# Scores of two heads at once in the two row halves of the array, in the first mixer of a three-mixer block

## The chip, the cores and the metric

The kernel runs on one core of a Trainium2 chip. A core has five engines that run side by side: TensorE (PE in the profile, with its weight loads as PEld), VectorE (DVE), ScalarE (ACT), GpSimd (POOL) and SyncE (SP), which here only issues DMAs. The metric is the device time of one execution in microseconds, lower is better.

## The reference

Two transformer blocks are chained over 512 tokens of width 1024, in float32. The change touches the first mixer alone, which has eight heads of forgetting attention ("fox") and eight heads of chunked attention with a relative bias ("chk"), all 64 wide. What it must compute per head:

```
def fox_attention(q, k, v, log_f):
    ...
        s = jnp.einsum('bqhd,bkhd->bhqk', qb, k).astype(jnp.float32) * scale
        s = s + cq[..., :, None] - cum[..., None, :]
        mask = k_pos[None, :] <= q_pos[:, None]
        p = jax.nn.softmax(jnp.where(mask, s, -jnp.inf), axis=-1)
        return jnp.einsum('bhqk,bkhd->bqhd', p.astype(v.dtype), v)
...
def even_mixer(h, w_in, b_forget, rel_bias, w_out):
    ...
    o = jnp.concatenate([o_a.reshape(b, s, W_FOX), o_b.reshape(b, s, W_CHK)], axis=-1)
    return o @ w_out
```

After it come a squared-ReLU MLP, a second mixer (stick-breaking and latent attention), a second MLP, a third mixer (differential and sparse attention) and a gated MLP. None of these is edited, but all share the planner that is described below.

## The kernel before, in words

Every float32 operand is kept as a pair: a high part, rounded to the short float format that TensorE takes, and a low part, the rest (`split`, one ScalarE and one VectorE instruction). A product of two pairs takes three matmuls: high by high, high by low, low by high. A matrix product `gemm` walks over weight blocks of 128 by 1024: a DMA brings the block (`wr`), `split` makes `wh` and `wl`, and 24 matmuls of 512 columns use it. These are the `psg<-h,wh` and `psg<-h,wl` rows; every matmul is preceded by its own weight load of 128 columns.

The first mixer works on pairs of heads. For each pair, `qk` makes q and k of both heads, each as one tile of 128 rows (head 0 in rows 0 to 63, head 1 in rows 64 to 127) by two parts by 512 tokens. For the scores, `to_stack` moves q by four DMAs into a tile `QS`, in which one head's high part stands in rows 0 to 63 and its low part in rows 64 to 127. `to_dup` moves k by four DMAs into two tiles `KK`, one for each head, with that head's k twice, one copy under the other. One matmul over 128 rows then adds two of the products, so that two matmuls (with k's high and low part) give a head's scores. Per head there are four of them in turn, for token blocks i = 0 to 3, with n = 128(i+1) columns.

`softmax` runs per block: VectorE adds the bias and takes the minimum (tile `x`), ScalarE does the exponential, VectorE the reciprocal, and GpSimd scales. `turn` transposes the four blocks on TensorE (`psp<-cst,x`), `av` multiplies by v (`pso<-pt,V`), and `fold` adds the two halves. The heads of a pair follow each other.

Nothing is issued in the order in which it is written. A `Recorder` notes every operation, `cost` gives each a price from a table, and `schedule` plays the five engines forward with these prices, with the buffers of each tile name (`BUFS`, `PBUFS`: two banks `s` for scores, three `g` for the products) and with priorities. The order that comes out is issued, so every instruction has the line of the issuing helper, L372, and groups are told apart by their tiles. TensorE runs its matmuls in that fixed order.

Pieces of later work (`fill`, `later`) stand between the steps of a pair, so that TensorE has matrix products to do while a softmax is on its way.

Of the kernel before, what the change touches and what calls it, by code (L numbers as in the profile page):

```python
# [14 lines left out]
AF = mybir.ActivationFunctionType  # L15
ALU = mybir.AluOpType
# [4 lines left out]
NT = 4  # L21
# [224 lines left out]
def size(ap):  # L246
    return math.prod(n for _, n in ap.ap[1:])


class Recorder:  # L250
# [71 lines left out]
    def cost(self, op):  # L322
        n = max(size(a) for a in op.acc[1] + op.acc[0])
        out = op.args[0]
        psum = any(str(a.space).endswith("PSUM") for a in op.acc[0])
        e = op.eng
        k = sum(isinstance(a, AP) for a in op.args[2:]) + sum(isinstance(a, AP) for a in op.kw.values())
        if op.name == "dma_start":
            return 450 if str(op.args[1].space).endswith("DRAM") else 625
        if e == "tensor":  # L330
            n = size(out)
            if op.name == "transpose":
                return 107
            if op.args[2].dtype == F32:
                return max(4 * n / 2.4, 428)
            return n / 2.4 + 2.5
        if e == "scalar":
            return 93 + 0.833 * n - (40 if psum else 0) + 93 * k
        if e == "vector":
            if op.name == "reciprocal":  # L340
                return 67 + 6.3 * n
            if op.name in ("memset", "tensor_copy") or (op.name == "tensor_scalar" and not psum):
                return 67 + 0.53 * n + 58 * k
            if op.name == "scalar_tensor_tensor":
                return 67 + 1.05 * n + 60 * (k - 1)
            return 67 + 1.05 * n
        if op.name == "tensor_scalar":
            return 160 + 0.836 * n + 83 * k
        if op.name == "affine_select":
            return 90 + 1.2 * n  # L350
        if op.name == "memset":
            return 36 + 0.83 * n
        return 958 if n <= 4 else 60 + 2.3 * n
# [37 lines left out]
    def schedule(self):  # L391
# [30 lines left out]
        while len(order) < len(ops):  # L422
            best = None
            for e in engs:
                if avail[e]:
                    s = clock[e]
                elif pend[e]:
                    s = max(clock[e], pend[e][0][0])
                else:
                    continue  # L430
                if best is None or s < best[0]:
                    best = (s, e)
            if best is None:
                raise RuntimeError("no instruction is ready: " + str({t: len(w) for t, w in waiting.items() if w}))
            now, e = best
            while pend[e] and pend[e][0][0] <= now:
                k = heapq.heappop(pend[e])[1]
                heapq.heappush(avail[e], (ops[k].prio, k))
            op = ops[heapq.heappop(avail[e])[1]]
            need = [t for t in op.tiles if t not in held]  # L440
            short = None
            for t in need:
                tag = self.tag[t]
                if not free[tag] or turn[t] != at[tag]:
                    short = tag
            if short is not None:
                waiting[short].append(op.n)
                continue
            late = max([free[self.tag[t]][0] for t in need], default=0.0)
            if late > now:  # L450
                heapq.heappush(pend[e], (late, op.n))
                continue
            for t in need:
                tag = self.tag[t]
                heapq.heappop(free[tag])
                held.add(t)
                at[tag] += 1
                for k in waiting[tag]:
                    heapq.heappush(pend[ops[k].eng], (now, k))
                waiting[tag] = []  # L460
            cost = op.cost
            if e == "tensor":
                stat = self.region(op.args[1])
                if stat != last:
                    cost = max(cost, 107)
                last = stat
            elif op.name == "activation" and TABLE.get(op.args[2], table) != table:
                table = TABLE[op.args[2]]
                cost += 1280
            end = now + cost  # L470
            clock[e] = end
            lat = self.LAT[e]
            if op.name == "tensor_tensor_reduce":
                lat = dict.fromkeys(lat, 425)
            if op.name == "dma_start":
                nbytes = 4 * math.prod(n for _, n in op.args[0].ap)
                dma = max(dma, end + 650) + nbytes / 360
                end = dma
            op.end = end
            order.append(op)  # L480
            for k in op.succ:
                o = ops[k]
                o.ready = max(o.ready, end + lat.get(o.eng, 0))
                o.left -= 1
                if not o.left:
                    heapq.heappush(pend[o.eng], (o.ready, o.n))
            for t in op.tiles:
                users[t] -= 1
                done_at[t] = max(done_at.get(t, 0.0), end + 200)
                if not users[t]:  # L490
                    tag = self.tag[t]
                    heapq.heappush(free[tag], done_at[t])
                    for k in waiting[tag]:
                        heapq.heappush(pend[ops[k].eng], (now, k))
                    waiting[tag] = []
# [7 lines left out]
class Net:  # L503
# [201 lines left out]
        self.nc.vector.tensor_tensor(x, ps, x, ALU.add)  # L705


    def scaled_pair(self, ps, rbc):
        t = self.tl("G", [128, 512])
        self.nc.vector.tensor_tensor(t, ps, rbc, ALU.mult)  # L710
        ab = self.pair("AB")
        self.split(ab, t)
        return ab

# [30 lines left out]
    def softmax(self, i, passes, bias, gate=None):  # L745

        nc = self.nc
        n = 128 * (i + 1)
        s = self.scores(i, passes)
        p = self.tl("x", [128, 512])  # L750
        m = self.small(4)
        nc.vector.tensor_tensor_reduce(p[:, :n], s[:, :n], bias(i), scale=1.0, scalar=3e38,
                                       op0=ALU.add, op1=ALU.min, accum_out=m[:, 0:1])
        nc.scalar.activation(p[:, :n], p[:, :n], AF.Exp, scale=-1.0, bias=m[:, 0:1], accum_out=m[:, 1:2])
        nc.vector.reciprocal(m[:, 2:3], m[:, 1:2])
        if gate == "raw":
            return p, m[:, 2:3]
        nc.gpsimd.tensor_scalar(p[:, :n], p[:, :n], m[:, 2:3], 1.0 if gate is None else gate(i), ALU.mult, ALU.mult)
        return p

    def turn(self, ps_list):

# [44 lines left out]
    def vhead(self, vt, u):  # L807
        return lambda j: vt[j][:, u].rearrange("p a d -> p (a d)")

    def qk(self, key, mov, rq, rk, tags="gg"):  # L810
        res = [None, None]

        def evac(m, ps):
            ab = self.scaled_pair(ps, rq if m == 0 else rk)
            res[m] = ab

        self.gemm(key, mov, evac, tags)
        return res
# [43 lines left out]
    def even_mixer(self):  # L862
        nc = self.nc
        rbc, rbcq = self.finish_norm([("rbc", 1.0), ("rbcq", -0.125)])
        h = self.h
# [6 lines left out]
        vt = self.v_tiles("fox_v0", h, self.rcol, gates, self.first)  # L872
# [6 lines left out]
        ps = self.psum("s")  # L879
# [36 lines left out]
        for kind, mk in (("fox", fox_bias), ("chk", chk_bias)):  # L916
            for t in range(4):
                if not (kind == "fox" and t == 0) and t % 2 == 0:
                    vt = self.v_tiles(f"{kind}_v{t // 2}", h, self.rcol)
                q, k = self.qk(f"{kind}_qk{t}", h, rbcq, rbc, "op" if kind == "fox" and t == 0 else "gg")  # L920
                qs = self.to_stack(q)
                kk = self.to_dup(k)
                if kind == "chk":
                    if t == 0:
                        half = self.out_part("out_ab0", ops[:4])
                    self.fill(half, OUT0[t], FILL0)
                ob = self.T()
                for u in range(2):
                    passes = [(qs[:, u], kk[u][:, 0]), (qs[:, u], kk[u][:, 1])]
                    self.soft_head(passes, mk(2 * t + u), self.vhead(vt, 2 * (t % 2) + u), ob, u)  # L930
                ops.append(self.finish_pair(ob))
        self.rec.flush()
        self.out_proj("out_ab1", ops[4:], "mlp0")
# [834 lines left out]
```

## Time and profile before

| what | value |
|---|---|
| median of 3 runs | 2084.16 us (2082.13 to 2088.24) |
| the profiled execution's own time | 2076.13 us |
| its span, first to last instruction | 2074.1 us |
| TensorE busy | 2017.1 us, 97% |
| VectorE, ScalarE, GpSimd busy | 55%, 43%, 19% |
| mean granted TensorE clock | 0.993 |

The profiled execution is 8 us shorter than the median of the timed runs, with 2 us of it outside the span. Matmul durations in the profile overlap, since a matmul is still draining when the next has begun; the pace of TensorE is therefore read from the distance between start times, not from durations.

### The profile page before, as it was taken

How to read it: one execution, taken by the hardware profiler on the slowest of the kernel's cores; microseconds unless marked ns; L12 is line 12 of the kernel's file. 1: busy time of each engine (PE TensorE's matmuls, PEld its weight loads, DVE VectorE, ACT ScalarE, POOL GpSimd, SP SyncE). 2: the span in 40 equal slices, each digit the busy share in tenths (PEclk: the TensorE clock that was granted, in tenths of full speed). 3: DMA queues.
4: the chain of work that ended last, by engine and by line, in shares of the span. 5: the costliest groups of instructions: out<-in, count | busy, mean ns of one | idle time of the engine just before them, and what ended most of it. 6: DMA issues, size and time to landing. Idle time of an engine off the chain costs nothing. (4 is left out here: it accounts for less than half of the span.)

```text
span 2074.1 us, 27228 instructions
## 1 busy us (share of the span) xinstructions
PE 2017.1 (97%) x9958; PEld 1683.7 (81%) x9958; DVE 1131.8 (55%) x2033; ACT 895.1 (43%) x1621; POOL 396.5 (19%) x524
## 2 busy tenths in 40 slices
PE   8999999999999999999999999989999999999998
PEld 7888878888888877778888888867788888888887
DVE  5667853434445576774434344766786644333334
ACT  5556542322335555653323243543685543222224
POOL 2343210000022463220000014211340221011013
PEclk9999999999999999999999999999999999999999
DMA  6445623333344315632333334473213222223232
GB/s 199 129 129 154 198 83 100 94 99 97 97 139 127 102 62 131 180 115 92 102 93 101 94 122 135 122 182 116 71 42 112 92 101 92 101 93 102 91 102 82
DMA packets 80293, 231.98 MB, mean 112 GB/s; under 512 B 11424, under 2 KB 15392, under 8 KB 80160
## 3 DMA queue, kind: packets, MB, share of 16 engines
q1 hardware_dynamic: 80160, 230.25, 36.8%
q8 instruction: 78, 1.28, 0.3%
q14 instruction: 55, 0.45, 0.1%
HBM read 183.04 MB, written 10.49 MB: 93 GB/s over the span
## 5 line engine op out<-in xcount | busy, mean ns | idle before, releaser
L372 PE MATMUL psg<-h,wh 128*128 128x512 f32 x2688 | 848.4, 393 | 0.9 <-ACT h L372 0.6
L372 ACT ACTIVATE wh<-wr 128x1024 fp32r<-128x1024 f32 (+3 forms) x313 | 326.3, 1042 | 846.0 <-PE psg L372 672.9
L372 PEld LDWEIGHTS psg<-h,wh 128*128 128x128 f32 x2688 | 503.3, 189 | 102.0 <-ACT h L372 1.5
L372 PE MATMUL psg<-h,wl 128*128 128x512 f32 x1344 | 528.9, 393 | 1.2 <-DVE wl L372 1.0
L372 DVE TENSOR_TENSOR wl<-wr,wh 128x1024 fp32r<-128x1024 f32 (+3 forms) x313 | 384.7, 1229 | 59.9 <-ACT wh L372 58.7
L372 PEld LDWEIGHTS psg<-h,wl 128*128 128x128 f32 x1344 | 253.6, 189 | 53.9 <-DVE wl L372 3.1
L372 PE MATMUL psg<-KK,wh 128*128 128x512 f32 (+1 forms) x788 | 237.8, 383 | 0.4 <-DVE V L372 0.2
L372 DVE TENSOR_TENSOR x<-psg,x 128x512 f32<-128x512 f32 (+1 forms) x120 | 78.2, 654 | 281.8 <-PE psg L372 281.7
L372 POOL TENSOR_TENSOR acc<-acc,T 128x512 f32<-128x512 f32 (+1 forms) x50 | 72.9, 1457 | 775.7 <-issue 627.3
L372 PE MATMUL psg<-V,wh 128*128 128x512 f32 (+1 forms) x672 | 205.7, 387 | 1.1 <-DVE G L372 1.1
L372 PEld LDWEIGHTS psg<-KK,wh 128*128 128x128 f32 x788 | 146.3, 188 | 29.5 <-ACT o L372 0.6
L372 PE MATMUL psg<-KK,wl 128*128 128x512 f32 (+1 forms) x394 | 150.8, 383 | 0.0
L372 PEld LDWEIGHTS psg<-V,wh 128*128 128x128 f32 x672 | 125.6, 188 | 27.3 <-ACT wh L372 1.2
L372 DVE SCALAR_TENSOR_TENSOR T<-psg,rbc 128x512 f32<-128x512 f32 x64 | 44.2, 691 | 167.2 <-PE psg L372 166.8
L372 ACT ACTIVATE x<-x,sm 128x128 f32<-128x128 f32 (+1 forms) x192 | 106.6, 558 | 54.7 <-DVE sm L372 53.9
L372 PE MATMUL psg<-V,wl 128*128 128x512 f32 (+1 forms) x336 | 129.9, 387 | 0.0
L372 PE MATMUL psg<-o,wh 128*128 128x512 f32 x384 | 126.2, 397 | 0.8 <-ACT wh L372 0.5
L372 PE MATMUL psg<-wh,h 128*128 128x256 f32 (+2 forms) x560 | 114.5, 292 | 6.6 <-ACT wh L372 6.6
L372 PE MATMUL pso<-pt,V 128*128 128x128 f32 (+3 forms) x432 | 108.8, 340 | 3.4 <-ACT pt L372 1.9
L372 POOL TENSOR_SCALAR x<-x,sm 128x128 f32<-128x128 f32 (+1 forms) x112 | 65.9, 594 | 174.6 <-DVE sm L372 122.8
L372 PEld LDWEIGHTS psg<-wh,h 128*128 128x128 f32 x560 | 92.4, 194 | 8.4 <-ACT wh L372 6.6
L372 POOL TENSOR_TENSOR T<-T,rbc 128x512 f32<-128x512 f32 x22 | 39.2, 1782 | 280.5 <-ACT T L372 280.5
(263 smaller groups left out, 2667.6 us busy)
## 6 DMA issues: line engine op xcount, KB each, us to landing
wr<-in_w_dram SPq DMA_DIRECT2D x302, 512.0 KB, 3.5
KK<-AB SPq DMA_DIRECT2D x48, 256.0 KB, 5.4
QS<-AB SPq DMA_DIRECT2D x48, 128.0 KB, 4.0
x<-xs SPq DMA_DIRECT2D x24, 256.0 KB, 3.3
xs<-P SPq DMA_DIRECT2D x16, 256.0 KB, 3.9
xs<-x SPq DMA_DIRECT2D x16, 256.0 KB, 2.0
h<-AB SPq DMA_DIRECT2D x16, 256.0 KB, 4.1
KK<-AB SPq DMA_DIRECT2D x32, 128.0 KB, 2.3
```

Of the source, the lines that this page charges most:

```text
L372: op.inst = getattr(getattr(nc, op.eng), op.name)(*op.args, **op.kw)
```

## The change

The stacked copies of q and k go. `qk` writes q's pair straight into a tile `QS` and k's into a tile `KK`, and each head's matmuls read their own 64 rows: head 0 rows 0 to 63, head 1 rows 64 to 127. Each token block then takes three matmuls over 64 rows per head instead of two over 128, written with the two heads in turn. Both heads' softmaxes are written side by side, with i from 3 down to 0, and share tiles `x`; the transposes of both heads come after them. The planner's prices change too: a matmul of pairs counts 32 columns' time beyond its own n columns where it counted 6, one over 64 rows counts half of that, and this holds for the whole program.

```diff
@@ cost
-            return n / 2.4 + 2.5
+            return (n + 32) / (4.8 if op.args[1].ap[0][1] == 64 else 2.4)
@@ schedule
-                    cost = max(cost, 107)
+                    cost = max(cost, 107 if op.args[1].ap[0][1] > 64 else 53)
@@ scaled_pair
-    def scaled_pair(self, ps, rbc):
+    def scaled_pair(self, ps, rbc, tag="AB"):
...
-        ab = self.pair("AB")
+        ab = self.pair(tag)
@@ new functions
+    HALF = ((0, 0), (0, 1), (1, 0))
+
+    def scores_two(self, i, q, k):
...
+        s = [self.psum("s"), self.psum("s")]
+        for a, (x, y) in enumerate(self.HALF):
+            for u in range(2):
+                r = slice(64 * u, 64 * u + 64)
+                nc.tensor.matmul(s[u][:, :n], q[r, x, 128 * i:128 * i + 128], k[r, y, :n], start=(a == 0), stop=(a == 2))
+        return s
...
+    def soft_pair(self, q, k, bias, v, dst):
...
+        P = [[None] * NT, [None] * NT]
+        bias = [b() for b in bias]
+        for i in (3, 2, 1, 0):
+            s = self.scores_two(i, q, k)
+            for u in range(2):
+                if i == 3:
+                    P[u][3] = self.tl("x", [128, 512])
...
+                self.soften(i, s[u], P[u][i], bias[u])
+        for u in range(2):
+            pt = self.turn(P[u])
+            o = self.psum("o")
+            self.av(o, pt, v[u])
+            self.fold(o, dst, u)
@@ qk
-    def qk(self, key, mov, rq, rk, tags="gg"):
+    def qk(self, key, mov, rq, rk, tags="gg", to=("AB", "AB")):
...
-            ab = self.scaled_pair(ps, rq if m == 0 else rk)
+            ab = self.scaled_pair(ps, rq if m == 0 else rk, to[m])
@@ even_mixer
-                q, k = self.qk(f"{kind}_qk{t}", h, rbcq, rbc, "op" if kind == "fox" and t == 0 else "gg")
-                qs = self.to_stack(q)
-                kk = self.to_dup(k)
+                q, k = self.qk(f"{kind}_qk{t}", h, rbcq, rbc, "op" if kind == "fox" and t == 0 else "gg", ("QS", "KK"))
...
-                for u in range(2):
-                    passes = [(qs[:, u], kk[u][:, 0]), (qs[:, u], kk[u][:, 1])]
-                    self.soft_head(passes, mk(2 * t + u), self.vhead(vt, 2 * (t % 2) + u), ob, u)
+                self.soft_pair(q, k, [lambda u=u: mk(2 * t + u) for u in range(2)],
+                               [self.vhead(vt, 2 * (t % 2) + u) for u in range(2)], ob)
```

`soften` is the old `softmax` without its scores and its tile: the same VectorE, ScalarE and GpSimd instructions.

How the planner's order moves shows best on TensorE in the last pair of heads of the mixer. There `psg` rows are the output product that fills in, and `pss` rows the scores. In the kernel before, the two matmuls of a token block stand together and all take 128 rows:

```order
L372 MATMUL pss_693<-KK_680,QS_679 128x128 x2
L372 MATMUL pss_696<-KK_680,QS_679 128x256 x2
L372 MATMUL psg_614<-o_357,wh_616 128x512
L372 MATMUL psg_614<-o_357,wl_617 128x512
L372 MATMUL psg_614<-o_430,wh_616 128x512 x2
L372 MATMUL pss_699<-KK_680,QS_679 128x384 x2
L372 MATMUL pss_702<-KK_680,QS_679 128x512 x2
```

In the changed kernel the same place, the widest block (n = 512, tile 649 for head 0 and 650 for head 1), reads so:

```order
L372 MATMUL pss_649<-KK_636,QS_630 128x512
L372 MATMUL pss_650<-KK_636,QS_630 128x512
L372 MATMUL psg_568<-o_339,wl_571 128x512
L372 MATMUL psg_568<-o_406,wh_570 128x512 x2
L372 MATMUL psg_568<-o_406,wl_571 128x512
L372 MATMUL psg_573<-o_191,wh_570 128x512 x2
L372 MATMUL pss_649<-KK_636,QS_630 128x512
L372 MATMUL pss_650<-KK_636,QS_630 128x512
L372 MATMUL pss_649<-KK_636,QS_630 128x512
L372 MATMUL pss_650<-KK_636,QS_630 128x512
L372 MATMUL psg_573<-o_191,wl_571 128x512
```

Here the heads alternate, as they are written, but 128-row products stand between the runs. At the other widths, the heads do not alternate. This is the first pair, also in the changed kernel, where tile 150 is head 0 and 151 head 1 at n = 384, and 158 and 159 the same at n = 256:

```order
L372 MATMUL pss_150<-KK_136,QS_130 128x384 x3
L372 MATMUL psg_192<-h_95,wh_194 128x512
L372 MATMUL psg_192<-h_95,wl_195 128x512
L372 MATMUL pss_151<-KK_136,QS_130 128x384 x3
L372 MATMUL psg_192<-h_97,wh_194 128x512 x2
L372 MATMUL psg_192<-h_97,wl_195 128x512
L372 MATMUL psg_192<-h_99,wh_194 128x512 x2
L372 MATMUL psg_192<-h_99,wl_195 128x512
L372 MATMUL pss_158<-KK_136,QS_130 128x256 x3
```

The three matmuls of one head stand together and those of the other head come later. Counted over the mixer, the changed kernel has 192 score matmuls in 64 runs with other matmuls between them: 10 runs in which the heads alternate (six of four matmuls, four of two), 4 lone ones at n = 512, and 50 runs of three or six, in each of which one head's matmuls of a width stand together.

On SP's queue the moves stood between the loads of weights, as here in the first pair of the kernel before (`wr` are weight blocks):

```order
L372 DMA QS_137<-AB_130 64x512 x2
L372 DMA wr_271<-in_w_dram 128x1024
L372 DMA QS_137<-AB_130 64x512 x2
L372 DMA wr_274<-in_w_dram 128x1024
L372 DMA KK_138<-AB_136 64x1024 x2
L372 DMA KK_139<-AB_136 64x1024 x2
```

In the changed kernel the `QS` and `KK` rows of the first mixer are gone from this queue and the `wr` rows follow each other.

## Rows read from the trace of the kernel before

**Rows 1.** The page: busy us of each engine, share of the span, instructions.
```profile
PE 2017.1 (97%) x9958; PEld 1683.7 (81%) x9958; DVE 1131.8 (55%) x2033; ACT 895.1 (43%) x1621; POOL 396.5 (19%) x524
```

**Rows 2.** Busy time by window; columns PE, PEld, DVE, ACT, POOL, clock, DMA share, GB/s.
```profile
29.00:266.00 237.00, 231.19 (x1309) 196.65 (x1308) 163.47 (x387) 131.75 (x296) 83.20 (x150) 1.00 0.55 152
...
280.00:640.00 360.00, 359.47 (x1637) 299.39 (x1636) 154.18 (x176) 118.87 (x152) 13.57 (x8) 1.00 0.32 101
```

**Rows 3.** What PE waited for in the first mixer, 29 to 266 us.
```profile
PE pss L372 <- DMA KK<-AB: 3.2, 3, 1.4
PE psp L372 <- POOL x L372: 1.3, 3, 0.8
PE pso L372 <- ACT pt L372: 0.6, 1, 0.6
PE psp L372 <- DVE pt L372: 0.2, 1, 0.2
PE psg L372 <- DVE wl L372: 0.2, 1, 0.2
```

**Rows 4.** PE in order of time, first mixer: start, us, tiles, rows*columns, shape.
```profile
223.28 0.70 PE L372 MATMUL pss<-KK,QS 128*128 128x128 f32 x4 [0.65 <-DMA KK<-AB]
223.81 0.40 PE L372 MATMUL psg<-o,wh 128*128 128x512 f32 x1
...
224.73 0.97 PE L372 MATMUL pss<-KK,QS 128*128 128x384 f32 x4
225.54 0.40 PE L372 MATMUL psg<-o,wl 128*128 128x512 f32 x1
```

**Rows 5.** PE in order of time, in the first MLP.
```profile
300.52 0.62 PE L372 MATMUL psg<-h,wh 128*128 128x512 f32 x2
300.97 0.39 PE L372 MATMUL psg<-h,wl 128*128 128x512 f32 x1
```

**Rows 6.** PE in order of time, third mixer: one 32-row matmul among 128-row ones.
```profile
1534.99 0.39 PE L372 MATMUL psg<-h,wh 128*128 128x512 f32 x1
1535.32 0.49 PE L372 MATMUL pso<-P,vcmp 32*128 32x512 f32 x1
1535.73 0.50 PE L372 MATMUL psg<-h,wl 128*128 128x512 f32 x1
1536.07 0.63 PE L372 MATMUL psg<-h,wh 128*128 128x512 f32 x2
```

**Rows 7.** PEld, the weight loads, at the same place.
```profile
1534.88 0.19 PEld L372 LDWEIGHTS psg<-h,wh 128*128 128x128 f32 x1
1535.31 0.18 PEld L372 LDWEIGHTS pso<-P,vcmp 32*128 32x128 f32 x1 [0.24 <-ACT x L372]
1535.73 0.19 PEld L372 LDWEIGHTS psg<-h,wl 128*128 128x128 f32 x1 [0.24 <-issue]
```

**Rows 8.** PE in order of time, third mixer: two 32-row matmuls together.
```profile
1517.35 0.45 PE L372 MATMUL pso<-pt,V 128*128 128x256 f32 x3
1517.73 0.73 PE L372 MATMUL pso<-P,vcmp 32*128 32x512 f32 x2
1518.39 0.98 PE L372 MATMUL psp<-cst,x 128*128 128x128 f32 x7
1519.13 0.48 PE L372 MATMUL pss<-X,rbcq 128*128 128x512 f32 x1
```

**Rows 9.** PE in order of time: two 62-row transposes among 128-row ones.
```profile
1449.34 0.38 PE L372 MATMUL psp<-cst,x 128*128 128x128 f32 x2
1449.65 0.33 PE L372 MATMUL psg<-cst,P 62*128 62x62 f32 x2
1449.92 0.44 PE L372 MATMUL psp<-cst,x 128*128 128x128 f32 x2
1450.11 0.48 PE L372 MATMUL pss<-KK,QS 128*128 128x512 f32 x1
```

**Rows 10.** The score matmuls of the first mixer, by their tile KK, to 280 us.
```profile
L372 PE MATMUL pss<-KK,QS x128: 220/336/497, 44.3 to 228.8; 128*128 128x128 f32 x32, 128*128 128x256 f32 x32, 128*128 128x384 f32 x32, 128*128 128x512 f32 x32
```

More of the change, by code (lines that the diff above doesn't have):

```diff
@@ L759, in softmax, with soften @@
         return p
+    HALF = ((0, 0), (0, 1), (1, 0))
+    def scores_two(self, i, q, k):
+        nc = self.nc
+        n = 128 * (i + 1)
+        s = [self.psum("s"), self.psum("s")]
[4 more added lines that the diff above has]
+        return s
+    def soften(self, i, s, p, bias):
+        nc = self.nc
+        n = 128 * (i + 1)
+        m = self.small(4)
+        nc.vector.tensor_tensor_reduce(p, s[:, :n], bias(i), scale=1.0, scalar=3e38,
+                                       op0=ALU.add, op1=ALU.min, accum_out=m[:, 0:1])
+        nc.scalar.activation(p, p, AF.Exp, scale=-1.0, bias=m[:, 0:1], accum_out=m[:, 1:2])
+        nc.vector.reciprocal(m[:, 2:3], m[:, 1:2])
+        nc.gpsimd.tensor_scalar(p, p, m[:, 2:3], 1.0, ALU.mult, ALU.mult)
+    def soft_pair(self, q, k, bias, v, dst):
[6 more added lines that the diff above has]
+                    P[u][3] = self.tl("x", [128, 512])
+                elif i == 2:
+                    t = self.tl("x", [128, 512])
+                    P[u][2], P[u][0] = t[:, 0:384], t[:, 384:512]
+                elif i == 1:
+                    if u == 0:
+                        t1 = self.tl("x", [128, 512])
+                    P[u][1] = t1[:, 256 * u:256 * u + 256]
+                self.soften(i, s[u], P[u][i], bias[u])
[4 more added lines that the diff above has]
+            self.fold(o, dst, u)
     def turn(self, ps_list):
```

## The prediction

> **What bounds the kernel now.** I read the page first. TensorE is busy 97% of the span and no other engine over 55% [rows 1], so what a change adds to or takes from TensorE's queue is what the end moves by, as long as TensorE has other work in its waits. Then the table of windows, to see whether that holds where the change is made. The first mixer, from 29 to 266 us, has TensorE busy for 231.19 of 237.00 us; in the MLP behind it, 359.47 of 360.00 [rows 2]. The reader is to see that only 5.8 us of this mixer are open. The list of waits says what they are: 3.2 us for the moves of k, and 1.3, 0.6, 0.2 and 0.2 us for GpSimd, ScalarE and VectorE [rows 3]. So 5.5 us is all that freeing TensorE from others can give here. The rest must come from its own pace, which I read from start times.
>
> **The third pass.** The mixer has 128 score matmuls over 128 rows, 32 of each width [rows 10]. In the order of time, four of them (two of 128 and two of 256 columns) take 223.81 - 223.28 = 0.53 us, and four of 384 and 512 take 225.54 - 224.73 = 0.81 us [rows 4]. A head thus needs 1.34 us, and sixteen heads 21.4 us. Half the rows do not halve a matmul's columns. With three matmuls per block where two stood, 192 at the same pace are 32.2 us: **+10.7 us**.
>
> **Two heads at a time.** What comes off this is only what the two row halves really do at once. No row of this trace has two matmuls in different halves next to each other, so I bound it. Nothing comes off, if they queue; at most, each neighbouring couple takes the time of one. The order of the changed kernel has ten alternating runs, six of four matmuls and four of two, all of 512 columns: 16 couples. The pace of a 512-column matmul is 0.225 us (two in 0.45 us) [rows 5], so the bounds are 0 and -3.6 us. With no row near either end I take the middle, **-1.8 us**. Everywhere else a head's three matmuls stand together, and one half of the array has nothing to do.
>
> **Going to 64 rows and back.** This is the largest term. The trace has a few matmuls over fewer rows. In the third mixer one over 32 rows and 512 columns stands among products of the same width. From the start of the matmul ahead of it to the start of the second one behind it, three matmuls take 1536.07 - 1534.99 = 1.08 us [rows 6]; at the usual pace they take 0.68 [rows 5]. So one excursion costs 0.40 us. The weight loads show how. For the 128-row product ahead, the load begins at 1534.88, 0.11 us before the matmul is marked as started. For the 32-row one it begins only at 1535.31, with its matmul, after 0.24 us in which the loader did nothing, and the same again for the 128-row one behind it [rows 6, 7]. The overlap of load and matmul is lost at both edges. Two 32-row matmuls together start and end in 1518.39 - 1517.73 = 0.66 us [rows 8] against 0.45, 0.21 us more, with the rest on their neighbours: the price is one per excursion, not one per matmul.
>
> Are 64 rows treated like 32? The nearest row in that sense is a couple of 62-row transposes. They and the four 128-row ones around them take 1450.11 - 1449.34 = 0.77 us [rows 9]. Seven ordinary transposes take 1519.13 - 1518.39 = 0.74 us [rows 8], 0.106 each, so six would take 0.63: 0.14 us more, or 0.24 if the narrow ones count half. That they too pay says that 62 rows are enough of a difference. The two prices per excursion bound it, 0.14 and 0.40 us. The score runs are wide matmuls among products, as in [rows 6], and I take 0.38. The Trainium skill, in "TensorEngine Tiling (Array Packing)", section "Tiling Modes", lists 64 rows by 128 columns as a mode of its own and says that changing the mode drains TensorE. By that rule all 64 runs pay and the whole sum is the one below; if 64 rows were no mode of their own it would be 24.3 us less. The trace agrees for 32 and 62 rows.
>
> The order of the changed kernel has the 192 matmuls in 64 runs, each with 128-row work on both sides. 64 x 0.38 = **+24.3 us** (bounds 9.0 and 25.6).
>
> **The moves.** Sixty-four DMAs go from SP's queue. What TensorE waited for them is 3.2 us [rows 3]: **-3.2 us**. The other 2.3 us of waits are for the softmax, whose VectorE, ScalarE and GpSimd instructions are the same in kind and number; I count them as staying, with -2.3 as a bound, since a TensorE that runs later waits less. The weight loads that stood between the moves on SP gain nothing: the weights' wait is 0.2 us in this mixer [rows 3].
>
> **Softmaxes side by side.** They cost nothing as long as products fill TensorE's queue meanwhile, which the order shows between the runs. Both score banks and both bias strips are now held by one pair, so TensorE could come to a block whose bank is still being read. That would cost, at each of 8 pairs, a wait like the longest for the moves, 1.4 us [rows 3]: a bound of +11 us.
>
> **The planner's prices elsewhere.** The later mixers are reordered a little. TensorE's whole idle time is 2074.1 - 2017.1 = 57 us [rows 1], of which some 12 lie in the start and the first mixer; I let a tenth of the other 45 go either way, 4.5 us, and count 0.
>
> **Sum.** 10.7 - 1.8 + 24.3 - 3.2 = +30.0 us. The profiled execution, 2076.1 us with 2 us around its span, becomes 2106. That execution lies 8 us under the median of the timed runs; I carry the difference over to the median, 2084.2 + 30 = **2114 us**, 1.4% slower.
>
> **Rivals.**
> *The halves do run at once and switching is free.* All 192 matmuls then count half: 16.1 us where 21.4 stood, -5.3, and with all waits gone -5.5 more: 2073 us, faster. Against it: the order sets couples next to each other in 16 places only, and [rows 6, 9] show a price. It decides only if TensorE holds a matmul back and pairs it over the products between, which a queue that runs in order does not show anywhere in this trace. The Trainium skill's same page, section "Overview", gives up to twice the speed for a contraction of 64 or less, which is this rival. No run so far shows it. 0.03.
> *Switching is free for 64 rows, but only the couples overlap.* 10.7 - 3.6 - 5.5 = +1.6: 2086 us, no change. For it: no 64-row matmul is in this trace. Against it: 62 rows pay [rows 9]. 0.07.
> *Switching costs the low price.* 10.7 - 1.8 + 9.0 - 3.2 = +14.7: 2099 us. For it: [rows 9] is the nearest in rows. 0.15.
> *The full price and waits for the banks on top.* 30 + 11: 2125 us. Against it: TensorE is later than the planner thinks, so the readers of the banks are early. 0.10.
> The forecast itself has 0.65.
>
> **The numbers.** A measurement of this kernel tells about 0.3%, 6 us, from no change. Slower by more: the forecast, the low price and the bank waits, 0.65 + 0.15 + 0.10 = 0.90. Same 0.07, faster 0.03. The range takes in the low price with 7 us of the other unknowns under it, and the bank waits with 4.5 us for the reordering above: 2092 to 2130.
>
> **What would show it.** In the first mixer, a run of three 64-row matmuls of 384 columns between products should take its 0.54 us and about 0.2 more, with another 0.2 on its neighbours, and weight loads should begin late at its edges. Alternating couples should take between 0.23 and 0.45 us. TensorE should wait for no DMA in the mixer, and the mixer should end some 30 us later, with the stages behind it as long as before. I would be wrong if 64-row runs start at the pace of their neighbours, or if the later mixers move by more than 5 us.

## The result and the profile after

The changed kernel takes 2116.47 us (median of 4, 2114.97 to 2118.95) where the kernel before takes 2084.32 (median of 4): 1.0165 times as long, 95% interval 1.0143 to 1.0186. The forecast was 2114, slower, in a range of 2092 to 2130. The time came out as said, but not for all of the reasons given: the first mixer lost less than the sum had it, and the planner's prices, which the sum had at nothing, lost about as much as all the rest of the change.

The page's busy line of the changed kernel, against [rows 1]:

```profile
PE 2053.2 (97%) x10022; PEld 1694.7 (80%) x10022; DVE 1132.1 (53%) x2033; ACT 898.9 (42%) x1621; POOL 394.0 (19%) x524
```

TensorE has 64 matmuls more and 36 us more that count as busy. The other engines have the same number of instructions as before. What TensorE waited for in the first mixer, from 21 to 296 us, against [rows 3]:

```profile
PE pss L372 <- POOL acc L372: 5.0, 1, 5.0
PE psg L372 <- DVE o L372: 0.6, 1, 0.6
PE psg L372 <- DVE wl L372: 0.3, 1, 0.3
```

The waits for the moves and for the softmax are gone, 5.3 of the 5.5 us in [rows 3]; waits for `wl` and `o`, 0.9 us, are listed in their place. The wait for the last sum of squares, at the end of the mixer and outside the window of [rows 3], has grown to 5.0 us. The same list of the kernel before has it with

```profile
PE pss L372 <- POOL acc L372: 1.5, 1, 1.5
```

Now the order of time, against [rows 4], with the start of each group ahead:

```profile
39.34 0.50 PE L372 MATMUL psg<-h,wl 128*128 128x512 f32 x1
39.78 0.73 PE L372 MATMUL pss<-KK,QS 64*128 64x512 f32 x4
40.44 0.73 PE L372 MATMUL psg<-h,wh 128*128 128x512 f32 x2
41.01 0.39 PE L372 MATMUL psg<-h,wl 128*128 128x512 f32 x1
41.24 0.40 PE L372 MATMUL psg<-h,wh 128*128 128x512 f32 x1
41.57 0.79 PE L372 MATMUL pss<-KK,QS 64*128 64x384 f32 x3
42.29 0.50 PE L372 MATMUL psg<-h,wh 128*128 128x512 f32 x1
42.62 0.40 PE L372 MATMUL psg<-h,wl 128*128 128x512 f32 x1
```

From 41.24 to 42.62 stand one product of 512 columns, three score matmuls of 384 and one more product: 1.38 us. At the usual pace they are 2 x 0.225 + 0.54 = 0.99. The run of 64-row matmuls costs **0.39 us** beyond its columns, as the 32-row one did in [rows 6]. The four of 512 columns, with the heads in turn, take 40.44 - 39.78 = 0.66 us, less than three products in a row (0.68) although they too pay for the way in: the two halves do work at once. The weight loads at the run of three, against [rows 7]:

```profile
41.01 0.19 PEld L372 LDWEIGHTS psg<-h,wh 128*128 128x128 f32 x1
41.56 0.47 PEld L372 LDWEIGHTS pss<-KK,QS 64*128 64x128 f32 x3 [0.36 <-DVE sm L372]
42.29 0.19 PEld L372 LDWEIGHTS psg<-h,wh 128*128 128x128 f32 x1 [0.25 <-issue]
```

At both edges the loader stands idle (0.36 and 0.25 us) and the load begins with its matmul, not ahead of it. The Trainium skill's rule that a change of mode drains TensorE ("TensorEngine Tiling (Array Packing)", section "Tiling Modes") agrees with this trace for 64 rows, at 0.39 us for the way in and out.

The later mixers lost too. Every norm begins with a small matmul `pss<-cst,acc` that marks where a stage ends. In the changed kernel, three of these starts:

```profile
294.37 1.73 PE L372 MATMUL pss<-cst,acc 128*128 128x1 f32 x8 [5.03 <-POOL acc L372]
...
647.14 1.05 PE L372 MATMUL pss<-cst,acc 128*128 128x1 f32 x8 [0.33 <-POOL acc L372]
...
949.90 1.87 PE L372 MATMUL pss<-cst,acc 128*128 128x1 f32 x8 [3.13 <-POOL acc L372]
```

The distances between such starts, in us, for the kernels of this study (the first column from the first norm at about 20.5 us; the last to the start of the last matmul; one profile each):

| kernel | prices | mixer 1 | MLP 1 | mixer 2 | MLP 2 | mixer 3 | rest |
|---|---|---|---|---|---|---|---|
| before | old | 249.1 | 351.8 | 293.1 | 348.9 | 440.0 | 362.8 |
| before, profiled again | old | 248.6 | 351.8 | 293.0 | 348.9 | 443.2 | 363.7 |
| changed | new | 273.8 | 352.8 | 302.8 | 352.9 | 443.0 | 363.2 |
| changed, old prices | old | 266.4 | 350.7 | 295.4 | 350.4 | 439.2 | 363.0 |
| before, new prices | new | 261.1 | 352.3 | 301.2 | 352.9 | 440.5 | 363.6 |
| zero rows | new | 257.6 | 352.9 | 300.5 | 351.3 | 442.9 | 363.2 |
| side by side alone | old | 257.6 | 350.7 | 292.1 | 348.9 | 442.5 | 363.0 |
| runs joined | new | 252.3 | 351.1 | 304.9 | 352.9 | 443.2 | 363.2 |
| joined, heads in turn | new | 251.2 | 353.0 | 303.0 | 352.4 | 439.0 | 363.2 |
| the same, old prices | old | 252.5 | 350.5 | 292.9 | 352.0 | 437.2 | 362.9 |
| two blocks a run | old | 251.2 | 351.1 | 292.8 | 348.9 | 436.3 | 362.9 |
| two blocks, low price | lower | 248.0 | 348.5 | 298.4 | 350.5 | 446.9 | 362.4 |
| before, low price | lower | 252.3 | 350.6 | 294.8 | 348.0 | 439.7 | 362.4 |
| before, high price | higher | 265.8 | 352.5 | 316.9 | 352.9 | 443.9 | 363.9 |

The two executions of the kernel before agree within 0.6 us in the first four stages, while mixer 3 differs by 3.1; differences of a few us there say nothing. The changed kernel lost 24.6 us in mixer 1, 9.7 in mixer 2 and some 4 in the second MLP. In mixer 2 TensorE's idle time rose from 19.1 to 25.4 us. The row that grew most in the list of waits there is for a move of the second mixer's own, which no edit touched; of the kernel before and then of the changed kernel:

```profile
PE pss L372 <- DMA QS<-AB: 1.9, 1, 1.9
```

```profile
PE pss L372 <- DMA QS<-AB: 4.6, 1, 4.6
```

### The profile page after: what moved, and what is told of

It reads as the page before. It is cut to its first block, busy times and chain, and to the rows that moved or that the text cites. A ratio compares the mean times of both kernels' runs of the same rounds, so it can differ in the third digit from the quotient of the medians.

```text
span 2117.0 us, 27110 instructions
## 1 busy us (share of the span) xinstructions
PE 2053.2 (97%) x10022; PEld 1694.7 (80%) x10022; DVE 1132.1 (53%) x2033; ACT 898.9 (42%) x1621; POOL 394.0 (19%) x524
## 5 line engine op out<-in xcount | busy, mean ns | idle before, releaser
L372 ACT ACTIVATE x<-x,sm 128x128 f32<-128x128 f32 (+3 forms) x192 | 106.7, 558 | 62.7 <-DVE sm L372 61.9
L372 POOL TENSOR_SCALAR x<-x,sm 128x384 f32<-128x384 f32 (+3 forms) x112 | 68.6, 618 | 210.4 <-DVE sm L372 177.7
```

Of the source, the lines that this page charges most:

```text
L372: op.inst = getattr(getattr(nc, op.eng), op.name)(*op.args, **op.kw)
```

## Experiments

Ratios are against the kernel before on the same chip, with 95% intervals. On these chips the kernel before took 2078.65, 2079.88 and 2078.62 us (medians), some 5 us less than the 2084 from which the expectations in us start, so the ratio is the fairer comparison.

**The prices of before in the changed kernel.**

```diff
-            return (n + 32) / (4.8 if op.args[1].ap[0][1] == 64 else 2.4)
+            return n / 2.4 + 2.5
...
-                    cost = max(cost, 107 if op.args[1].ap[0][1] > 64 else 53)
+                    cost = max(cost, 107)
```

> The changed kernel with the planner's prices of before, so that the later mixers are ordered nearly as before; the first mixer still has 64-row score matmuls, in 61 runs. Theory A (0.40 us for each run of 64-row matmuls, and the new prices cost something in the later mixers, whose stages are 18 us longer in the profile): 2098 to 2108 us, the first mixer ends as late as in the changed kernel (294 us), and the stages behind it take what they took before. Rival (the later stages differ only from one execution to the next, and all the loss is in the first mixer): 2114 to 2118 us.

Measured: 2092.61 us, 1.0077 (1.0059 to 1.0096). The time is below theory A's range; by the ratio, which makes 2100 us of 2084, it is inside. The prices are about half of the loss: 1.0165 less 1.0077. Mixer 2 is back at 295.4 us. Mixer 1 is at 266.4 and not at 273.8, which theory A had not said: the prices cost 7 us there too. All of the change but the prices (the third pass, the 64-row runs, the moves that go, the softmaxes side by side) loses 17.3 us in mixer 1. The only wait left in its list is 2.6 us for the last sum of squares.

**The new prices in the kernel before.**

```diff
-            return n / 2.4 + 2.5
+            return (n + 32) / (4.8 if op.args[1].ap[0][1] == 64 else 2.4)
```

(and the second price line as in the change)

> The kernel before with nothing changed but the planner's prices. Theory A: the later mixers lose, 2092 to 2102 us, with the first mixer ending near 270 us. Rival (prices don't matter): 2082 to 2088 us.

Measured: 2099.15 us, 1.0102 (1.0085 to 1.0119), no change to any operation. Theory A was right that they cost, wrong that mixer 1 is spared (261.1 us where before has 249.1). What TensorE waited for in it, from 10 to 2050 us, the largest rows:

```profile
PE pss L372 <- POOL acc L372: 8.8, 5, 4.5
PE pss L372 <- DMA KK<-AB: 6.5, 5, 2.6
PE psg L372 <- DVE wl L372: 6.0, 8, 1.8
PE pss L372 <- DMA QS<-AB: 4.6, 1, 4.6
PE pss L372 <- DVE sm L372: 4.6, 6, 1.5
```

In the kernel before, the same list has for these:

```profile
PE pss L372 <- POOL acc L372: 3.4, 3, 1.7
PE pss L372 <- DMA KK<-AB: 3.2, 3, 1.4
PE psg L372 <- DVE wl L372: 2.3, 5, 1.0
```

I read this as: matmuls that depend on a DMA or on another engine now come too early in TensorE's queue. It is not all of the loss. The profiled span is 25.5 us longer; TensorE's idle time makes 13.7 of that (57.0 to 70.7), and the rest is in time that counts as busy, with the same 9958 matmuls at a mean granted clock of 0.989 where before has 0.993.

**More of the same, both ways.** The kernel before, with the pair matmul at `0.9 * n / 2.4` (192 ns at 512 columns) and at `(n + 64) / 2.4` (240 ns), where before has 216 and the change 227.

> The kernel before with TensorE's pair matmuls priced lower than before (0.9 x n columns, 192 ns at 512 where before had 216 and the change 227). Theory B (a planner that thinks TensorE faster puts more other work ahead of each dependent matmul, so the waits shrink): faster than before, 0.992 to 0.998, and the second mixer under 293 us. Rival (the old price happens to suit this program and any other loses): 1.003 to 1.010.

> The kernel before with the same matmuls priced higher still (n + 64 columns, 240 ns at 512). Theory B: slower than with the change's prices, 1.012 to 1.020, with more waits for DMAs and for the last sum of squares. Rival (no order in it): anywhere from 1.000 to 1.010.

Measured: low 0.9995 (0.9978 to 1.0012), high 1.0207 (1.0185 to 1.0228). With 192, 216, 227 and 240 ns the ratio goes 0.9995, 1, 1.0102, 1.0207. Upwards theory B has the direction, with a loss just above its range; downwards it missed (0.992 to 0.998 expected, mixer 2 at 294.8 us and not under 293): there is nothing left to gain. In the high kernel, over the same stretch:

```profile
PE pss L372 <- POOL acc L372: 10.1, 6, 4.8
PE pss L372 <- DMA KK<-AB: 7.0, 5, 1.8
PE psg L372 <- DVE wl L372: 6.0, 10, 1.6
PE pss L372 <- DMA QS<-AB: 5.3, 2, 4.7
```

A true price for TensorE (512 columns take 0.225 to 0.227 us) makes a worse plan than one that is too low. That the low price had given slack to everything else in the plan is my reading of it; no run tests it by itself.

**Score matmuls of a block kept together.** The planner gets a rule that the six matmuls become ready together, once both score banks are free.

```diff
+    def together(self, got):
+        mine = {o.n for o in got}
+        deps = set().union(*(o.deps for o in got)) - mine
+        tiles = set().union(*(o.tiles for o in got))
+        for o in got:
+            o.deps = o.deps | deps
+            o.tiles = set(tiles)
...
```

(`schedule`'s test for free buffers, which now takes two banks at once, is left out here.) In one kernel the loop over heads is outside (all three of head 0, then of head 1), in the other inside, as in the change. Prices are the new ones. The order that is issued has the six of a run as written, in every run of both.

> The changed kernel, with the six score matmuls of a token block kept together in the order (33 runs instead of 64), first all three of head 0, then all three of head 1. Same matmuls, same prices. Theory A (price per run): 31 runs less at 0.40 us, -12.4, and 16 couples that no longer alternate, +3.4: 2105 to 2110 us. Rival (a price for each 64-row matmul, or for each change of head): no gain, 2116 to 2120 us.

> As the kernel with joined runs (33 runs), but with the two heads in turn within each run, so that all 192 matmuls stand in 96 couples. Theory A with overlap of the halves: -12.4 for the runs and about -5 for 80 more couples, of which the narrow ones gain little because each still needs its weights loaded: 2095 to 2102 us. Rival (the halves don't really work at once, their starts are only marked together): same as the joined runs, 2105 to 2112 us. In both, no better than the kernel before.

Measured: 2095.77 us, 1.0086 (1.0068 to 1.0103), and 2094.64 us, 1.0086 (1.0067 to 1.0105). Mixer 1 fell from 273.8 to 252.3 and 251.2 us. Of the first 21.5 us, 13.2 are edges of runs and 9.0 couples, in the way of counting of the next section; the gaps grew by 0.7. A price for each matmul or for each change of head is out. But with the heads one after the other it gained as much as with the heads in turn, which neither theory had. A run of six in the first of these (head 0 three times, then head 1 three times in the program):

```profile
40.45 0.40 PE L380 MATMUL psg<-h,wh 128*128 128x512 f32 x1
40.78 0.80 PE L380 MATMUL pss<-KK,QS 64*128 64x384 f32 x6
41.51 0.50 PE L380 MATMUL psg<-h,wh 128*128 128x512 f32 x1
```

and in the other, with the heads in turn:

```profile
41.23 0.79 PE L380 MATMUL pss<-KK,QS 64*128 64x384 f32 x6
41.94 0.50 PE L380 MATMUL psg<-h,wl 128*128 128x512 f32 x1
```

Six matmuls take 0.73 and 0.71 us from the start of the run to the product behind it; in the changed kernel three of the same width took 42.29 - 41.57 = 0.72. The second head is free in either order. Single records show these six starting as three couples, 10 ns apart in the first kernel and 2 to 8 in the second.

The changed kernel has two runs of six that show the same, and there the widths tell the heads apart. Head 1's three of 256 columns are issued first, then head 0's three of 128:

```profile
161.99 0.61 PE L372 MATMUL pss<-KK,QS 64*128 64x256 f32 x6
162.53 0.50 PE L372 MATMUL psg<-h,wl 128*128 128x512 f32 x1
```

The single records start at 161.99 (256 columns), 162.00 (128), 162.17 (128), 162.22 (256), 162.28 (128) and 162.33 (256). The six take 0.54 us, and three of 256 columns alone take the same (45.25 to 45.79).

**Three passes over all rows.** Each head's q gets a tile of 128 rows with zeros in the other head's rows.

```diff
...
+            for u, z in enumerate(res[m]):
+                r, other = slice(64 * u, 64 * u + 64), slice(64 - 64 * u, 128 - 64 * u)
+                self.nc.gpsimd.memset(z[other].bitcast(F32), 0.0)
+                self.split(z[r], t[r])
...
-                nc.tensor.matmul(s[u][:, :n], q[r, x, 128 * i:128 * i + 128], k[r, y, :n], start=(a == 0), stop=(a == 2))
+                nc.tensor.matmul(s[u][:, :n], q[u][:, x, 128 * i:128 * i + 128], k[:, y, :n], start=(a == 0), stop=(a == 2))
```

> The changed kernel, new prices, but each head's q stands in its own tile of 128 rows in which the other head's rows are zero, so that the three score matmuls take all 128 rows: the third pass without 64-row runs and without overlap. It adds a ScalarE and a VectorE instruction per pair and two fills of zeros on GpSimd. Theory A (0.40 us for each of the 64 runs): 25 us less for the runs, some 7 more for matmuls that no longer overlap, 1.008 times the kernel before. Rival (the runs cost nothing and the third pass and the prices make all the loss): 1.016 as in the changed kernel.

Measured: 2099.99 us, 1.0105 (1.0086 to 1.0124). Mixer 1 is 16.2 us shorter than in the changed kernel; 18 were expected of it. The ratio is above the 1.008 expected and clear of the rival's 1.016. The same 192 matmuls in 61 runs cost less over all rows than over half of them, as theory A says. By the count of the next section 26.4 us of edges are gone, the couples' 3.8 us are lost, and there are 6.7 us more of waits and gaps, as the order differs too: the planner has these matmuls at the full price.

**Softmaxes side by side alone.** The kernel before, with `soft_pair` over its stacks.

```diff
+        for a in range(2):
+            for u in range(2):
+                nc.tensor.matmul(s[u][:, :n], q[:, u, 128 * i:128 * i + 128], k[u][:, a, :n], start=(a == 0), stop=(a == 1))
...
```

(left out: the prices of before, and `to_stack` and `to_dup` put back)

> The kernel before with its stacks, moves, 128-row scores and prices, but with the two heads' softmaxes side by side, i from 3 to 0, as in the change. The prediction's step (it costs nothing): 0.997 to 1.003 times the kernel before. Rival (two banks and two strips held by one pair make TensorE wait): up to 11 us, 1.005.

Measured: 2085.05 us, 1.0032 (1.0015 to 1.0048), mixer 1 at 257.6 us. What TensorE waited for from 21 to 280 us:

```profile
PE pss L372 <- DMA KK<-AB: 4.9, 6, 1.3
PE pss L372 <- issue: 4.5, 4, 2.6
PE pss L372 <- POOL acc L372: 2.6, 1, 2.6
PE pss L372 <- DVE sm L372: 2.4, 4, 0.9
```

It is not free while the moves are there. More of the scores wait for a move (6 waits where before has 3, 1.7 us more). Of the 2.4 us for `sm`, which VectorE writes as it reads a score bank, 2.0 are waits of scores; they fit the rival. For the 4.5 us of `issue` the profile shows no releaser, so their cause stays open. In the changed kernel the moves are gone, and its list has none of these waits.

**Joined runs with the prices of before.** Heads in turn, in 34 runs, with both price lines of before.

> The joined runs with the heads in turn (34 runs), with the planner's prices of before. If the prices cost what they cost alone (1.010 for the kernel before with the new ones), this takes the joined runs from 1.0086 to 0.998 to 1.001 times the kernel before, with the later mixers as long as before and the first mixer at 242 to 248 us where the kernel before has 249. Rival (the new prices suit the 64-row kernel and only hurt the old one): 1.006 or more.

Measured: 2078.51 us, 0.9995 (0.9979 to 1.0010). The total is where theory A had it, with mixer 2 back at 292.9 us; mixer 1 stayed at 252.5 us, above the 242 to 248 expected. The price effect is mostly in mixer 2 here (303.0 to 292.9 us), not in mixer 1.

**Two blocks in a run.** Blocks 2 and 0 share one bank per head (384 + 128 columns), so `for blocks in ((3,), (2, 0), (1,))`, 26 runs; and the same with the low price (29 runs).

> As the joined runs with the prices of before, but token blocks 2 and 0 share a score bank and one run, so 26 runs instead of 34. Theory A: 8 runs less at 0.40 us, 3.2 us less than the joined runs with old prices, 0.996 to 0.9995 times the kernel before. Rival (the longer run holds a bank longer and TensorE waits for it): no gain over the joined runs.

> Two token blocks in a run, with the low price. Theory B: 0.990 to 0.997 times the kernel before, a version that beats both. Rival: 1.002 or more.

Measured: 0.9998 (0.9984 to 1.0013) and 0.9987 (0.9966 to 1.0008). Mixer 1 went from 252.5 to 251.2 us, not by 3.2, and TensorE waited 3.4 us for GpSimd's scaled probabilities and 3.5 for the last sum of squares, where the joined runs had 0.5 and 1.5. That is no gain over the joined runs, as the rival said, though neither is a wait for a bank. With the low price mixer 1 is at 248.0 us, but mixer 2 at 298.4, and the total misses theory B's 0.990 to 0.997. No version here is measurably faster than the kernel before.

**The kernel before once more**, unchanged, one profile.

> The kernel before, unchanged, profiled once more, to see how much a stage varies between executions of the same program. Theory A (the planner's prices move the second mixer from 293 to between 300 and 305 us): the second mixer takes 290 to 296 us again and the first mixer, from its first norm to the next, 247 to 251 us. Rival (stages differ by 8 us or more from one execution to the next): a second mixer near 300 us or a first mixer near 257 us.

Measured: mixer 1 248.6 us, mixer 2 293.0 us, 2079.27 us in all. The stages that the argument rests on, mixers 1 and 2 and the second MLP, repeat.

## Why the prediction was right, and where it was not

Mixer 1 can be taken apart with the trace. For each matmul I take the distance to the next start and subtract (n + 32)/2.4 ns, the pace that 512 columns (0.227 us) and 256 columns (0.120 us) show in the products. What is left is put to couples that started within 20 ns, to the edges of 64-row runs (the step into a run, those within it, the step out and the one behind), or to all else. The kernel before has 27.3 us of "all else". The changed kernel with the prices of before stands beside it, since 7 us of the changed kernel's mixer 1 are the prices' work:

| term | forecast | before to changed | before to changed with old prices |
|---|---|---|---|
| third pass | +10.7 | +9.3 | +9.2 |
| edges of the runs | +24.3 | +26.4 (64 runs, 0.41 each) | +24.4 (61 runs, 0.40 each) |
| two heads at a time | -1.8 | -3.8 (18 couples) | -4.4 (22 couples) |
| waits and other gaps | -3.2 | -7.3 (27.3 to 19.9) | -11.8 (27.3 to 15.4) |
| mixer 1 | +30.0 | +24.6 (249.1 to 273.8) | +17.3 (249.1 to 266.4) |
| later stages | 0 | +7 by the medians, +18 by the two profiles | -1 by the ratio, +3 by the two profiles |
| whole | +30 | +32 by the medians | +16 by the ratio |

- **Third pass: right.** The formula gives 128 columns 0.067 us, which is too little: in the kernel before, score matmuls of 128 columns ahead of one of 512 take 0.109 to 0.113 us to its start. With 0.11 the term is 16 x 0.63 = +10.1 us. The place in [rows 4], just behind a wait, gives 0.145 for this width.
- **Going to 64 rows and back: right**, in mechanism and size. The price of 0.38 us per run, from a 32-row row, became 0.41; the low price of the 62-row transposes and the case of free switching are out.
- **Two heads at a time: right in kind, mis-sized.** I took the middle between nothing and all. It is all: a couple takes the time of one. The 50 runs in which each head's matmuls stand together have few couples, so it gave only 3.8 us. Joined runs have 94 couples and give 13 us.
- **The moves: mis-sized.** I counted 3.2 us and left 2.3 as a bound. Of the 5.5 us of listed waits 5.3 went, and with the prices of before all gaps together fell by 11.8 us. I read this as a TensorE that is late: with the runs it falls behind the plan, and what it used to wait for is ready. The kernel with three passes over all rows fits that: it has no moves and no 64-row runs, and 26.6 us of gaps. With the new prices 4.5 us of the gain were given back; the wait for the last sum of squares is 5.0 us there, 2.6 with the old prices, 1.5 before.
- **Side by side at nothing: right in the change**, as far as its list of waits tells, and only there. With the moves kept it cost 0.3%.
- **The planner's prices elsewhere at 0, with 4.5 us either way: wrong.** This is the step that failed. The new prices alone cost 1.0% in the kernel before, and 1.0165 less 1.0077 in the changed one. I had taken a tenth of the idle time as what a new order could move; mixer 2 alone moved by 9.7 us, more than the 5 us that the prediction named as a sign of being wrong. And I had looked for it in the later stages only: mixer 1 holds 7 us of it.

The second MLP, 4.0 us longer, is a case by itself. The table of windows over its first 15 us gives the stretch and its length, the busy time and instructions of PE, PEld, DVE, ACT and POOL, the granted clock, the DMA share and GB/s. First the kernel before, then the changed kernel (and 2 us of that stretch), the changed kernel with old prices, and the joined runs with old prices:

```profile
914.69:929.69 15.00, 15.00 (x72) 12.56 (x73) 7.14 (x9) 8.15 (x12) 1.02 (x1) 1.00 0.30 99
```

```profile
949.90:964.90 15.00, 15.00 (x58) 12.61 (x59) 5.38 (x7) 5.80 (x9) 1.02 (x1) 0.77 0.19 65
...
952.00:954.00 2.00, 2.00 (x6) 1.52 (x6) 0.00 (x0) 0.00 (x0) 1.02 (x1) 0.50 0.00 0
```

```profile
933.56:948.56 15.00, 15.00 (x65) 12.38 (x66) 5.72 (x8) 6.65 (x10) 1.02 (x1) 0.89 0.31 98
```

```profile
916.00:931.00 15.00, 15.00 (x58) 12.62 (x59) 5.39 (x7) 6.01 (x9) 1.03 (x1) 0.77 0.23 73
```

In part of the stretch TensorE runs at 1.2 GHz, a granted clock of 0.50. With old prices the MLP takes 348.9 us at a clock of 1.00, 350.4 at 0.89 and 352.0 at 0.77; with new prices 351.3 at 0.89 (three passes over all rows) and 352.9 at 0.77. So some 3.1 of the 4.0 us go with the clock and 0.9 with the prices. Why the clock fell is open. TensorE waited 1.7 us for the sum ahead of this MLP in the kernel before and 3.1 in the changed one, but also 1.7 in the two kernels with old prices where the clock fell.

So the total was hit by luck. Without the new prices the change cost about 16 us where I had 30, mostly because 11.8 us of gaps went where I had counted 3.2; the new prices, which I had at 0, put about as much on top again. The difference between the two profiled executions is 43 us, not 32: the first profile of the kernel before was a short one of its kind, 8 us under the median, as the prediction noted.

What stays open: why a lower price gains nothing more; why in the joined runs the price hardly matters to mixer 1 (251.2 us with the new, 252.5 with the old); and which of the two price lines hurts the changed kernel, since they were always moved together there.

## What to carry to other kernels

Work in one half of the rows paid at each way from whole to half and back, here 0.4 us; so count the runs in the order that is really issued, not the matmuls, and keep both halves' work together in one run, in whichever order. A price table that sets an order is part of the kernel: correct prices for one engine alone can make the plan worse, and an edit to them should be timed by itself. A forecast that comes out right in total should be checked stage by stage before it is believed.

## What was not expected of the hardware

- In a run of 64-row matmuls the second head's first one starts 10 ns after the first head's first, although two more of the first head stand between them in the program (six of 384 columns in 0.73 us, three alone in 0.72). In the changed kernel a matmul of 128 columns on one half started 10 ns after the first of three of 256 on the other half, with the two others issued ahead of it (162.00 and 161.99 us). TensorE thus started a matmul on the free half ahead of earlier ones that wait for the other half. The Trainium skill's "TensorE: Matmul & The Clock Gate", section "Part 3: Packing small matmuls — row/col tiling" (on what overlaps), says that matmuls keep program order, strictly first in, first out; these runs differ, and the measurement decides. So the words ahead of the prediction, that TensorE runs its matmuls in the fixed order of the plan, hold for whole rows and within a half, but not between the halves. No run shows a pairing across 128-row products.
- The couples are nearly free even at the narrow widths: six matmuls of 128 columns take 0.49 us from their start to the product behind them, in the first of the joined kernels from 47.32 to 47.81 us; a run of three of them in the changed kernel takes 0.47 (50.22 to 50.69).
